# Eight subtractions given to GpSimd, and one weight rounding moved by a few products

## The chip, the core and the metric

The kernel runs on one core of one Trainium2 chip. The metric is the device time of one execution in microseconds (us). The kernel before took 1075.73 us, the median of three runs (1075.58 to 1076.07).

## What is computed

One encoder layer on 1024 tokens of width 1024, all in float32. A normed input goes through one combined projection into two kinds of attention; their outputs are normed and projected; then comes a gated feed-forward with a small convolution over the tokens, and a last norm. Cut to what matters:

```
hn = rmsnorm(h, norm_mix)
qa, ka, va, qb, kb, vb = split(hn @ w_in)
o_a = window_gqa_sink(rope(qa), rope(ka), va, sink)      # |i-j| <= 128, 8 heads
o_b = neighbourhood_attention(qb, kb, vb, rpb)           # 16 x 64 grid, 8 heads
h  = h + concat(rmsnorm(o_a, norm_a), rmsnorm(o_b, norm_b)) @ w_out
hn = rmsnorm(h, norm_ffn)
g  = conv3(hn @ w_gate) + conv_b
h  = h + (silu(g) * (hn @ w_up)) @ w_down
out = rmsnorm(h, norm_final)
```

## The kernel before

Everything lies transposed: features on the 128 partitions, tokens along a row. A tile of 128 features by 1024 tokens is worked on in two halves of 512 tokens.

**Split numbers.** Each float32 operand of a matmul is split into a high half (`whi`, `ph`, the first half of `hg`), which ScalarE rounds by a copy, and a low half (`wlo`, `pl`, the second half of `hg`), which VectorE forms as the original minus the high half. A product then takes three matmuls: high weight by high input, high weight by low input, low weight by high input (`block`, L169 to L172; `group`, L957 to L961). In the feed-forward a group of four feature tiles makes 12 matmuls. The low weight is read by the third matmul of each three (L961).

**TensorE's order is written out by hand** (`manual_schedule`, L128): its instructions run in the order of the code. On the other engines a scheduler orders the instructions when the program is built, with help from priorities and from `issue_after` (`behind`, L145). Each engine then works through its own queue strictly in order: an instruction that waits holds up all that stand behind it. SyncE's queue (SP) issues most loads.

**Attention.** Projections of the normed input, 18 tiles of 128 columns (`Project`), run as a filler between the attention steps: `rest` (L744) is a generator that yields after each `block`, and the attention loop draws on it at set rates. A tile's weights come as two raw tiles of four blocks. The first is rounded in `load` (L558), at the start of the tile before. The second is rounded in `load_rest` (L562); `rest` calls it for the next tile when the running tile has done `REST` = 11 further blocks (L757). The tiles are rounded by `halve_w` (L158): one ScalarE copy (L162) and one VectorE subtraction (L163). For the last tile, m = 17, `halve_w` gets `held`, so that both are issued behind the softmax weights' latest split (marks "high" and "rest", L417 and L418). This tile takes its eight blocks in another order (L575 to L581): for each k both token halves, so it yields 16 times and needs the second four weights from its ninth block on. After it come the eight tiles of the output projection's first part (`OutA`), which begin with rounding their own weights.

In the attention steps VectorE, ScalarE and GpSimd share the softmax: VectorE adds the bias and takes the row's minimum (L403), ScalarE takes the exponential (L407), GpSimd scales (L411), TensorE transposes (L517), ScalarE and VectorE split the result (L417, L418), and TensorE multiplies by the values (L528, L529). GpSimd also prepares the bias tiles (L481, L482).

**Feed-forward.** Gate and up projections are computed for feature tiles `f` (`Gated`, L1090) by a scheme of Strassen's kind: seven products in place of eight, on sums of the 2 x 2 blocks of weights and of the normed input. The input's blocks are (feature tiles 0 to 3 or 4 to 7) by (first or second 512 tokens); `at(k, h)` is feature tile k, half h. The products are `p1` and `p2` (plain blocks), `p5`, `p6`, `p3`, `p7` (sums "s1", "s2", "s4", "s3" of the weights) and `p4` ("22"). The input's sums are formed in place in `at(k, 0)` and `at(k, 1)` of the tiles 0 to 3:

```
B["t1"]:  sub(at(k, 1), at(k, 1), at(k, 0))       # L1181, read by p5
B["t2"]:  sub(at(k, 1), at(k + 4, 1), at(k, 1))   # L1191, read by p6
t3:       sub(at(k, 0), at(k, 1), at(k, 0))       # L1198, read by p7
t4:       sub(at(k, 1), at(k + 4, 0), at(k, 1))   # L1199, read by p4
```

Each sum is split by `operand` (L963 to L968: a ScalarE copy, L966, and a VectorE subtraction, L967). The fourth sum overwrites the second, so it has to wait until the second's operand has been formed. `sub` (L998) is a VectorE subtraction of 128 x 512 elements.

The first four units (`HEAD`, L1170 to L1220) run product by product: all p5, all p6, all p3, all p7, all p4. Their weight sums are formed in turn (`head_weights`, L1002, with `sub` too) and rounded by `split_w` (L943: ScalarE copy L948, VectorE subtraction L949). Results leave the accumulators by VectorE (L1110 for p5, L1117 for p6, L1121 for p3, L1134 for p7, L1139 for p4), and the convolution takes a ScalarE pass and two VectorE passes per unit (L1127 to L1130). Raw weights come through three buffers, rounded weights through nine (L946, L953). From the fifth unit on a loop (L1290) does the seven products of one unit after the other, with the next unit's weights prepared step by step (`Weights`, L1045).

The loop is followed by the down projection, again by seven products, and the final norm, in which GpSimd takes two of the tiles (L1384).

Of the kernel before, what the change touches and what calls it, by code (L numbers as in the profile page):

```python
# [16 lines left out]
ALU = mybir.AluOpType  # L17
# [22 lines left out]
REST = 11  # L40
# [13 lines left out]
def hybrid_layer(tc, xT, w_first, w_in, w_out, w_gate, w_up, w_down, small, sink, rpb, consts, rope, out):  # L54
    nc = tc.nc
    with ExitStack() as ctx:
# [88 lines left out]
        def behind(*names):  # L145

            stack = ExitStack()
            for n in names:
                stack.enter_context(tc.issue_after(mark[n].ins))
            return stack  # L150
# [7 lines left out]
        def halve_w(raw, held=False):  # L158

            hi, lo = (wpool.tile([128, 4, 128], F32R, name=n, tag=n) for n in ("whi", "wlo"))  # L160
            with behind(*["high", "rest"] * held):
                mark["weights"] = nc.scalar.activation(hi, raw, AF.Copy)  # L162
                mark["weights low"] = nc.vector.tensor_tensor(lo, raw, f32(hi[:, :, :]), op=ALU.subtract)  # L163
            return [(hi[:, j, :], lo[:, j, :]) for j in range(4)]
# [389 lines left out]
        class Project:  # L554
# [5 lines left out]
                self.w = halve_w(raw)  # L560

            def load_rest(self):  # L562
                self.w += halve_w(self.raw, self.m == 17)

            def run(self):
                self.t = tmp("t")
# [50 lines left out]
        xg, first = [None] * KT, [Project(m) for m in range(3)]  # L617
        third = first[2]
        jobs = [Project(m) for m in range(3, 18)] + [OutA(d) for d in range(KT)]

        def split_x(k, part=slice(0, S)):

            g, src = col(C_NMIX + k), xts[k][:, part]
            hi, lo = (t[:, part] for t in xg[k])
            pin(nc.scalar.activation(hi, src, AF.Copy, scale=g))
            pin(nc.vector.scalar_tensor_tensor(lo, src, g, f32(hi), op0=ALU.mult, op1=ALU.subtract))  # L626
# [54 lines left out]
        for part in range(3):  # L681
            for p, ps in zip(first, banks):
                w, x = p.w[0], xg[0]
# [38 lines left out]
        def make_stacks(job):  # L722
            with tc.high_priority(offset=400):
                stacks(job.m, job.t)
            done.add(job.m)

        def settle(age):

            for item in list(later):
                item[0] -= 1  # L730
                if item[0] <= 0:
                    later.remove(item)
                    item[1]()
            while waiting and (len(waiting) > 1 or age >= (LATE if waiting[0].m == 3 else SOON if waiting[0].m == 17 else LAG)):
                m = waiting[0].m
                if live["op"] + needs(m) > slots["op"]:
                    break
                live["op"] += needs(m)
                with behind(*["stack", "low"] * (m == 3)):
                    waiting.pop(0).post()  # L740
# [3 lines left out]
        def rest():  # L744
            for i, job in enumerate(jobs):
                if i + 1 < len(jobs):
                    with behind(*[["spread", "root"], ["stack"]][i] if i < 2 else []):
                        jobs[i + 1].load()
                for n, _ in enumerate(job.run()):
                    yield True  # L750
                    if i == 0:
                        if n == 8:
                            with behind("copied"):
                                for p in first[:2]:
                                    make_stacks(p)
                        continue
                    if n == REST and i + 1 < len(jobs):  # L757
                        jobs[i + 1].load_rest()
                    settle(n)
                    if (i, n) in aux:  # L760
                        aux[i, n]()
                if i == 0:
                    with behind("stack", "copied"):
                        jobs[1].load_rest()
                    with behind("weights", "weights low"):
                        make_stacks(third)
                if isinstance(job, Project):
                    waiting.append(job)
                while len(waiting) > 2:
                    settle(0)  # L770
                    if len(waiting) > 2:
                        yield False
# [29 lines left out]
        for i in range(8):  # L802
            aux[13, 1 + i + i // 2] = normed_a(*divmod(i, 2))
        filler = rest()
        live["op"] = sum(needs(m) for m in range(3))

# [115 lines left out]
        for h in range(2):  # L922
            wide = widen(vb2[h], "pt")
            for i in range(4):
                x = mix[4 + i][:, tsl(h)]
# [48 lines left out]
        at = lambda k, h: h1[k][:, tsl(h)]  # L974
# [20 lines left out]
        HEAD = 4  # L995
        FH = FT // 2
        FO = [f for k in range(FH) for f in (k, k + FH)]
        sub = lambda o, x, y: nc.vector.tensor_tensor(o, x, y, op=ALU.subtract)  # L998

        wsum = [fpool.tile([128, 4, 128], F32, name="ws", tag="tt", bufs=6) for _ in range(HEAD)]  # L1000

# [193 lines left out]
            head_weights(i, "s2")  # L1195
        B[2, 2] = [operand(at(k, 1), "op") for k in K2]
        for k in K1:
            sub(at(k, 0), at(k, 1), at(k, 0))  # L1198
            sub(at(k, 1), at(k + 4, 0), at(k, 1))  # L1199
        for i, u in enumerate(units):  # L1200
            u.p6()
            head_weights(i, "s4")
# [212 lines left out]
        for i, (p, j, c) in enumerate(order):  # L1415
# [4 lines left out]
            f, n = PARTS[c]  # L1420
# [146 lines left out]
```

## Time and profile before

| | |
|---|---|
| median of 3 runs | 1075.73 us |
| the profiled execution | 1076.77 us, of which the span of its instructions is 1075.0 us |
| busy: TensorE | 1063.8 us (99% of the span) |
| VectorE | 867.3 us (81%) |
| ScalarE | 555.7 us (52%) |
| GpSimd | 106.8 us (10%) |
| mean granted TensorE clock | 0.997 |

How the views are read. A row of the timeline has the start, the duration, the engine (PE is TensorE, PEld its weight loads, DVE is VectorE, ACT ScalarE, POOL GpSimd, SP SyncE), the line, the operation, what it writes and reads with shapes, how often it follows itself, and in brackets the engine's idle time before it and what ended it. Matmuls are pipelined: their starts tell the pace, not their durations. VectorE's instructions overlap a little as well: a subtraction of 128 x 512 lasts 0.69 us and the next one starts 0.60 us after it. A row of the waits has who waited for whom, the total in us, how often, and the longest. A row of a window has the busy time of TensorE, of its weight loads, of VectorE, ScalarE and GpSimd in that stretch, each with its number of instructions, then the granted clock, the share of time the DMA engines moved data, and GB/s. A row of the groups has how often, the busy time and the mean in ns, then the idle time before. A row of the DMA issues has how many, their size, and the median us from issue to landing.

### The profile page before, as it was taken

How to read it: one execution, taken by the hardware profiler on the slowest of the kernel's cores; microseconds unless marked ns; L12 is line 12 of the kernel's file. 1: busy time of each engine (PE TensorE's matmuls, PEld its weight loads, DVE VectorE, ACT ScalarE, POOL GpSimd, SP SyncE). 2: the span in 40 equal slices, each digit the busy share in tenths (PEclk: the TensorE clock that was granted, in tenths of full speed). 3: DMA queues.
4: the chain of work that ended last, by engine and by line, in shares of the span. 5: the costliest groups of instructions: out<-in, count | busy, mean ns of one | idle time of the engine just before them, and what ended most of it. 6: DMA issues, size and time to landing. Idle time of an engine off the chain costs nothing.

```text
span 1075.0 us, 14902 instructions
## 1 busy us (share of the span) xinstructions
PE 1063.8 (99%) x5094; PEld 889.6 (83%) x5094; DVE 867.3 (81%) x1596; ACT 555.7 (52%) x1059; POOL 106.8 (10%) x188
## 2 busy tenths in 40 slices
PE   9999999999999999999999999999999999999997
PEld 7888888888888888887788888888888888888887
DVE  7889887768878799899988877887887858897765
ACT  8457776647676554534434343432434645544451
POOL 1124333222332000000000000000000000000002
PEclk9999999999999999999999999999999999999998
DMA  7223122322234245214342232322222788867644
GB/s 278 74 74 80 40 69 60 89 69 79 78 88 148 96 156 210 78 56 162 135 157 98 106 110 81 129 106 108 98 89 101 251 288 308 270 216 241 222 139 157
DMA packets 68220, 144.94 MB, mean 135 GB/s; under 512 B 8240, under 2 KB 18736, under 8 KB 68144
## 3 DMA queue, kind: packets, MB, share of 16 engines
q1 hardware_dynamic: 57920, 118.69, 34.9%
q10 hardware_dynamic: 10224, 25.30, 6.2%
q8 instruction: 40, 0.66, 0.2%
q14 instruction: 36, 0.29, 0.1%
HBM read 103.58 MB, written 28.57 MB: 123 GB/s over the span
## 4 chain that ended last, share of the span: by engine, by line
PE 89%; DVE 7%; ACT 1%; issue 1%; DMA 1%; POOL 0%; SPq 0%; DVEq 0%; ACTq 0%
PE pj L170 8%; PE pj L172 8%; PE pj L171 8%; PE dn L959 7%; PE dn L961 7%; PE dn L960 7%; PE z L961 5%; PE z L959 5%; PE z L960 5%; PE s L381 3%; PE x L959 3%; PE x L961 3%; PE x L960 3%; PE y L961 3%; PE y L959 3%; PE y L960 3%
## 5 line engine op out<-in xcount | busy, mean ns | idle before, releaser
L948 ACT ACTIVATE whi<-ws 128x512 fp32r<-128x512 f32 (+1 forms) x100 | 60.3, 623 | 126.8 <-DVE ws L1066 82.5
L959 PE MATMUL dn<-xd,whi 128*128 128x512 f32 (+1 forms) x330 | 124.0, 376 | 0.0
L961 PE MATMUL dn<-xd,wlo 128*128 128x512 f32 (+1 forms) x330 | 123.7, 375 | 0.0
L960 PE MATMUL dn<-xd,whi 128*128 128x512 f32 (+1 forms) x330 | 123.7, 375 | 0.0
L961 PE MATMUL z<-hg,wlo 128*128 128x512 f32 x264 | 103.1, 390 | 0.9 <-DVE wlo L949 0.7
L170 PE MATMUL pj<-xgh,whi 128*128 128x512 f32 x245 | 103.3, 422 | 0.0
L959 PE MATMUL z<-hg,whi 128*128 128x512 f32 x264 | 103.0, 390 | 0.0
L960 PE MATMUL z<-hg,whi 128*128 128x512 f32 x264 | 102.8, 389 | 0.0
L407 ACT ACTIVATE p<-p,nm 128x385 f32<-128x385 f32 (+3 forms) x128 | 75.2, 587 | 50.8 <-DVE nm L403 49.7
L411 POOL TENSOR_SCALAR p<-p,sm 128x384 f32<-128x384 f32 (+1 forms) x128 | 78.1, 622 | 207.2 <-DVE sm L409 171.7
L171 PE MATMUL pj<-xgl,whi 128*128 128x512 f32 x245 | 96.2, 393 | 0.3 <-DVE xgl L626 0.3
L172 PE MATMUL pj<-xgh,wlo 128*128 128x512 f32 x245 | 96.4, 393 | 0.0
L949 DVE TENSOR_TENSOR wlo<-raw,whi 128x512 fp32r<-128x512 f32 (+1 forms) x102 | 66.4, 671 | 26.6 <-ACT whi L948 25.6
L418 DVE TENSOR_TENSOR pl<-pt,ph 128x384 fp32r<-128x384 f32 (+2 forms) x108 | 63.5, 589 | 24.9 <-ACT ph L417 23.5
L948 ACT ACTIVATE whi<-raw 128x512 fp32r<-128x512 f32 (+1 forms) x102 | 60.5, 612 | 44.6 <-DMA raw<-in_w_down_dram 19.8
L949 DVE TENSOR_TENSOR wlo<-ws,whi 128x512 fp32r<-128x512 f32 (+1 forms) x100 | 67.0, 683 | 19.1 <-ACT whi L948 17.9
L1384 POOL TENSOR_TENSOR h<-h,wide 128x256 f32<-128x256 f32 (+1 forms) x6 | 5.4, 918 | 707.4 <-ACT wide L1380 707.4
L417 ACT ACTIVATE ph<-pt 128x384 fp32r<-128x384 f32 (+2 forms) x108 | 55.2, 512 | 32.4 <-PE pt L517 24.7
L961 PEld LDWEIGHTS dn<-xd,wlo 128*128 128x128 f32 x330 | 62.1, 188 | 11.2
L960 PEld LDWEIGHTS dn<-xd,whi 128*128 128x128 f32 x330 | 62.1, 188 | 11.2
L959 PEld LDWEIGHTS dn<-xd,whi 128*128 128x128 f32 x330 | 62.1, 188 | 10.9
L1274 ACT ACTIVATE xd<-xd 128x512 fp32r<-128x512 f32 x77 | 47.6, 626 | 43.8 <-DMA xd<-x 42.1
(270 smaller groups left out, 2678.0 us busy)
## 6 DMA issues: line engine op xcount, KB each, us to landing
xd<-x SPq DMA_DIRECT2D x77, 256.0 KB, 4.8
raw<-in_w_down_dram SPq DMA_DIRECT2D x72, 256.0 KB, 3.8
raw<-in_w_gate_dram SPq DMA_DIRECT2D x22, 512.0 KB, 3.5
raw<-in_w_up_dram SPq DMA_DIRECT2D x22, 512.0 KB, 3.9
x<-c ACTq DMA_DIRECT2D x22, 512.0 KB, 3.3
raw<-in_w_in_dram SPq DMA_DIRECT2D x30, 256.0 KB, 2.8
raw<-in_w_down_dram SPq DMA_DIRECT2D x36, 192.0 KB, 4.2
x<-t ACTq DMA_DIRECT2D x11, 512.0 KB, 2.7
```

Source lines behind the costliest of these rows:

```text
L170: nc.tensor.matmul(ps, w[0], x[0][:, tsl(h)], start=first, stop=False)
L171: nc.tensor.matmul(ps, w[0], x[1][:, tsl(h)], start=False, stop=False)
L172: nc.tensor.matmul(ps, w[1], x[0][:, tsl(h)], start=False, stop=last)
L407: nc.scalar.activation(p[:, j, 0:e], p[:, j, 0:e], AF.Exp, bias=nm, scale=-1.0, accum_out=sm[:, j:j + 1])
L411: nc.gpsimd.tensor_scalar(p[:, i, 0:m], p[:, i, 0:m], sm[:, i:i + 1], 1.0, op0=ALU.mult, op1=ALU.mult)
L417: mark["high"] = nc.scalar.activation(ph[:, 0:n], ps[:, 0:n], AF.Copy)
L418: mark["rest"] = nc.vector.tensor_tensor(pl[:, 0:n], ps[:, 0:n], f32(ph[:, 0:n]), op=ALU.subtract)
L948: nc.scalar.activation(hi, src, AF.Copy)
L949: nc.vector.tensor_tensor(lo, src, f32(hi[:, :, :]), op=ALU.subtract)
L959: nc.tensor.matmul(ps, w[0], x[0], start=first and i == 0, stop=False, skip_group_check=True)
L960: nc.tensor.matmul(ps, w[0], x[1], start=False, stop=False, skip_group_check=True)
L961: nc.tensor.matmul(ps, w[1], x[0], start=False, stop=last and i == len(ws) - 1, skip_group_check=True)
```

## The change

Two edits that have nothing to do with each other. The third and fourth sums of the normed input, eight subtractions, are issued on GpSimd instead of VectorE. And the second weights of the last projected tile (m = 17, `jobs[14]`) are rounded when that tile has done three of its own blocks (n = 2), no longer at the twelfth block of the tile before it, and without the `held` order.

```
             def load_rest(self):
-                self.w += halve_w(self.raw, self.m == 17)
+                self.w += halve_w(self.raw)
...
         jobs = [Project(m) for m in range(3, 18)] + [OutA(d) for d in range(KT)]
+        last_in = jobs[14]
...
-                    if n == REST and i + 1 < len(jobs):
+                    if n == REST and i + 1 < len(jobs) and jobs[i + 1] is not last_in:
                         jobs[i + 1].load_rest()
+                    if n == 2 and job is last_in:
+                        job.load_rest()
                     settle(n)
...
-        sub = lambda o, x, y: nc.vector.tensor_tensor(o, x, y, op=ALU.subtract)
+        sub = lambda o, x, y, engine=nc.vector: engine.tensor_tensor(o, x, y, op=ALU.subtract)
...
         for k in K1:
-            sub(at(k, 0), at(k, 1), at(k, 0))
-            sub(at(k, 1), at(k + 4, 0), at(k, 1))
+            sub(at(k, 0), at(k, 1), at(k, 0), nc.gpsimd)
+            sub(at(k, 1), at(k + 4, 0), at(k, 1), nc.gpsimd)
```

Besides, the scheduler places the instructions around both edits anew: VectorE's, ScalarE's and SyncE's queues differ from the kernel before near them, and in the feed-forward up to the seventh unit or so. TensorE's order is the same.

## The prediction

> Line numbers are those of the kernel before; times are us from the start of the profiled span.
>
> **What bounds the kernel now.** I read the page's first part, then TensorE's waits in the two stretches that the diff touches.
>
> ```profile
> PE 1063.8 (99%) x5094; PEld 889.6 (83%) x5094; DVE 867.3 (81%) x1596; ACT 555.7 (52%) x1059; POOL 106.8 (10%) x188
> ```
>
> ```profile
> PE o L529 <- DVE pl L418: 0.9, 1, 0.9
> ```
>
> ```profile
> PE z L961 <- DVE wlo L949: 0.7, 2, 0.4
> PE y L961 <- DVE wlo L949: 0.5, 2, 0.3
> ```
>
> The first wait row is 250 to 320 (attention), the others are 440 to 540 (the head of the feed-forward). TensorE is busy 99% of the span, so only its pauses can be won. What the pauses cost is read from TensorE's starts (timeline):
>
> ```profile
> 453.40 0.39 PE L959 MATMUL y<-hg,whi 128*128 128x512 f32 x1
> ...
> 464.28 0.39 PE L959 MATMUL z<-hg,whi 128*128 128x512 f32 x1
> ...
> 486.04 0.39 PE L959 MATMUL z<-hg,whi 128*128 128x512 f32 x1
> ...
> 494.40 0.39 PE L961 MATMUL z<-hg,wlo 128*128 128x512 f32 x1
> 494.71 0.50 PE L959 MATMUL z<-hg,whi 128*128 128x512 f32 x1
> 495.05 0.40 PE L960 MATMUL z<-hg,whi 128*128 128x512 f32 x1
> 495.78 0.50 PE L961 MATMUL z<-hg,wlo 128*128 128x512 f32 x1 [0.34 <-DVE wlo L949]
> 496.12 0.39 PE L959 MATMUL z<-hg,whi 128*128 128x512 f32 x1
> ...
> 532.73 0.39 PE L959 MATMUL z<-hg,whi 128*128 128x512 f32 x1
> ```
>
> From 453.40 to 464.28 are four products of 12 matmuls: 10.88, so 2.72 a product and 0.227 a matmul. From 486.04 to 532.73 are 16 products, 43.53 at that pace; they took 46.69. So this stage loses 3.16, in five pauses like that at 495: the wait, and about 0.2 besides, since the steps around it are 0.31 and 0.34 instead of 0.227. Each pause waits for a low half of a weight from VectorE. VectorE has no idle time in front of them, where the sums stand, and little between them:
>
> ```profile
> 465.00:470.00 5.00, 5.00 (x24) 4.14 (x23) 5.00 (x9) 3.07 (x5) 0.00 (x0) 1.00 0.00 0
> 495.00:500.00 5.00, 4.66 (x21) 3.49 (x20) 4.13 (x8) 2.07 (x4) 0.00 (x0) 1.00 0.62 192
> ```
>
> (After the colon and the sum: TensorE, weight loads, VectorE 5.00 of 5.00, ScalarE, GpSimd idle, clock 1.00.)
>
> **The sums: what goes.**
>
> ```profile
> 453.90 1.89 DVE L998 TENSOR_TENSOR h<-h,h 128x512 f32<-128x512 f32 x3
> 455.70 1.89 DVE L967 TENSOR_TENSOR hg<-h,hg 128x512 fp32r<-128x512 f32 x3
> 457.51 0.69 DVE L998 TENSOR_TENSOR h<-h,h 128x512 f32<-128x512 f32 x1
> ...
> 464.71 0.70 DVE L1110 TENSOR_TENSOR c<-y,c 128x512 f32<-128x512 f32 x1
> 465.31 1.30 DVE L998 TENSOR_TENSOR h<-h 128x512 f32<-128x512 f32 x2
> ...
> 470.13 0.70 DVE L1117 TENSOR_TENSOR gs<-z,c 128x512 f32<-128x512 f32 x1
> ```
>
> The eight sums (L1198, L1199) stand from 465.31 to 470.13: 4.82, or 0.60 each. VectorE would gain 4.8 if nothing else changed, more than any single pause.
>
> **What comes.** Eight instructions on GpSimd, of a kind that the trace shows at this size:
>
> ```profile
> L1384 POOL TENSOR_TENSOR h<-h,wide 128x512 f32<-128x512 f32 x2 | 2.6, 1296 | 691.9 <-ACT wide L1380 691.9
> ```
>
> They take 1.30 each, 10.4 in all. GpSimd is empty until that row, so nothing queues behind them there. In the changed program's order the first three need only the second sums (453.90 on), so GpSimd starts near 455, not at 465: beside VectorE's work, not after it. What that does is shown where GpSimd's L481 and L482 met VectorE in attention:
>
> ```profile
> 248.17 0.99 POOL L481 TENSOR_TENSOR xb<-cst,rr 128x384 f32<-128x384 f32 x1 [1.18 <-DVE nm L403]
> 249.12 1.17 POOL L482 TENSOR_TENSOR xb<-cst,rr 128x256 f32<-128x256 f32 x1
> ```
>
> ```profile
> 248.22 1.50 DVE L163 TENSOR_TENSOR wlo<-raw,whi 128x512 fp32r<-128x512 f32 x1
> 249.63 1.21 DVE L299 SCALAR_TENSOR_TENSOR kb<-t,cst,ka 128x512 fp32r<-128x512 f32 x1
> ```
>
> And the same forms where they did not meet (the last row is for the rounding, below):
>
> ```profile
> 294.55 0.99 POOL L481 TENSOR_TENSOR xb<-cst,rr 128x384 f32<-128x384 f32 x1 [0.37 <-DVE nm L403]
> 295.50 0.72 POOL L482 TENSOR_TENSOR xb<-cst,rr 128x256 f32<-128x256 f32 x1
> ```
>
> ```profile
> 295.57 0.54 DVE L418 TENSOR_TENSOR pl<-pt,ph 128x384 fp32r<-128x384 f32 x1
> ...
> 301.51 0.69 DVE L163 TENSOR_TENSOR wlo<-raw,whi 128x512 fp32r<-128x512 f32 x1
> ...
> 306.29 0.42 DVE L418 TENSOR_TENSOR pl<-pt,ph 128x256 fp32r<-128x256 f32 x1 [0.83 <-ACT ph L417]
> ```
>
> L163 took 1.50 instead of 0.69 and ended 0.56 after L481's end; L482 then took 1.17 instead of 0.72 and ended 0.57 after L163; L299 ended 0.55 after L482. They went strictly in turn. An instruction on GpSimd holds VectorE up for its own time less 0.15 (0.72 against 0.57). L418, which reads PSUM, ran at 0.54 beside L482: it wasn't held.
>
> So a sum on GpSimd costs a VectorE instruction with both inputs in SBUF 1.30 - 0.15 = 1.15. That is dearer than the 0.60 which it removes. From 455.10 VectorE has 17 instructions up to 465.31, all but four (L1110, which read PSUM) with two inputs in SBUF. Taken in turn: GpSimd 455.05 to 456.20, VectorE to 456.75, and so on, eight rounds of 1.15 + 0.55, with two of L1110 beside GpSimd. VectorE comes to the place of 465.31 at 465.31 + 8 x 1.15 - 2 x 0.60 - 8 x 0.05 (0.55 against 0.60) = 472.9, say 473.0, against 470.13 now: **2.9 late instead of 4.8 early**. Bounds: 465.3 if no instruction is held, 474.5 if L1110 is held too.
>
> The Trainium skill, page "SBUF — State Buffer", section "Who interferes with whom", states that VectorE and GpSimd share a port pair as an exclusive lock, taken by a VectorE instruction with two SBUF inputs against a GpSimd instruction that reads SBUF, and that the later one blocks fully. The trace agrees on the turns (0.56, 0.57 and 0.55 behind each other) and differs on the length: by the page's wording the whole 1.30 would be held, 1.2 more over eight sums, and the time would be 1079.9; by the rows it is 1.15.
>
> **What is late then.** I walk the changed program's order with 0.60 for an instruction, 1.20 for each conv pass (L1128, L1129) and 0.76 from a VectorE start to the matmul that reads it:
>
> ```profile
> 495.05 0.68 DVE L949 TENSOR_TENSOR wlo<-ws,whi 128x512 fp32r<-128x512 f32 x1
> ```
>
> (its matmul: 495.78 above). Weights come back by
>
> ```profile
> raw<-in_w_gate_dram SPq DMA_DIRECT2D x22, 512.0 KB, 3.5
> ...
> raw<-in_w_up_dram SPq DMA_DIRECT2D x8, 256.0 KB, 3.1
> ```
>
> 1. The second sums' last low half (L1192, k = 3) stands behind seven of the holds: it ends at 466.95 and is readable at 467.05; its matmul is due at 464.28 + 10 x 0.227 = 466.55: 0.5 lost. On ScalarE's queue the same operand's high half stands behind three copies that now wait for GpSimd (third sums 0 and 1, fourth sum 0, the last done at 461.3); its own input comes at 463.6, so that new wait hides.
> 2. Fifteen instructions from 473.0 bring VectorE to the first s3 weight sum (L1015) at 482.0. The low halves of the third sums stand among them and find GpSimd done (468.2): no wait. From there to the third unit's s3 low half stand twelve instructions of 0.60 and four conv passes of 1.20, and two waits: 0.9 until the second unit's raw weights are there (buffer free at 482.7, 3.1 to load), 0.3 for ScalarE. 482.0 + 7.2 + 4.8 + 1.2 = 495.2, readable at 495.95. TensorE's s3 products (L1133) start at 486.04 + 0.5 = 486.6; the third unit's needs it at 486.6 + 2 x 2.72 + 0.45 = 492.5: 3.45 lost. The fourth unit's is due at 498.7 and comes at 498.95: 0.25.
> 3. The next unit's gate weights start to load when the buffer of a "22" weight is free, at 501.7, and land at 505.2; VectorE stands behind them for 1.9. The walk brings it to the low half of the second loop unit's s1 at 532.65, readable at 533.4, due at 531.55: 1.85.
>
> Lost: 0.5 + 3.45 + 0.25 + 1.85 = 6.05, and 0.2 for each of four pauses, 6.85. Now 3.16 is lost. The sums cost **+3.7**. After that unit the walk finds every low half ready, as the trace of before does up to the kernel's end part. If VectorE were only 1 late at 473, item 2 would shrink by 1.9.
>
> **The rounding.** It moves one ScalarE copy and one VectorE subtraction (L162, L163), no DMA. In the changed order they follow the first output weights' rounding, near 307 and 308.3. Now the copy stands at 300.85 and the subtraction at 301.51 (above):
>
> ```profile
> 300.85 0.62 ACT L162 ACTIVATE whi<-raw 128x512 fp32r<-128x512 f32 x1
> ...
> 304.05 0.96 ACT L417 ACTIVATE ph<-pt 128x384 fp32r<-128x384 f32 x2
> ```
>
> ```profile
> 304.14 0.38 PE L517 MATMUL pt<-cst,p 128*128 128x128 f32 x2
> 304.59 0.44 PE L528 MATMUL o<-ph,v 128*128 128x384 f32 x1
> 305.18 0.44 PE L529 MATMUL o<-pl,v 128*128 128x384 f32 x1
> 305.46 0.38 PE L517 MATMUL pt<-cst,p 128*128 128x128 f32 x2
> ```
>
> From 304.14 to 305.46 is 1.32; two transposes of 0.11 and two of 0.18 are 0.58. So 0.74 goes, because ph (304.05) leaves before the second exponential instead of behind it. In the new place VectorE's 0.83 of idle time at 306.29 covers the subtraction, and the weights are needed only eight blocks of three matmuls into that tile, 5.4 after its start. On SP one output-weight load moves behind a q copy; it belongs to the second output tile, a whole tile later. If that cover failed, up to 0.7 would come back. The 0.9 pause at 286 is another instruction's and stays.
>
> Sum: 1076.77 (span 1075.0 and 1.77 around it) + 3.7 - 0.7 = 1079.8; against the median 1075.73: **1078.7**.
>
> **Rivals.** *No collision* (faster): the sums run beside VectorE at no price. Then it is 4.8 early from 465 on, the 3.16 go, and 1075.73 - 3.16 - 0.74 = 1071.8; half of it, 1073.5. It decides if a hold costs under 0.60; for it speaks only a meeting like 295.57, where VectorE read PSUM. Chance 0.15. *Collision absorbed*: VectorE loses 1 to 3, but the new order brings critical halves earlier, and the pauses stay near 3 to 4: 1075 to 1076.5. For it: VectorE idles 0.87 in 495 to 500. Chance 0.2. *Deeper delay*: L1110 is held too (474.5), and each later load starts later; 1.5 more at three places, 1082 to 1083. Chance 0.1. That the rounding isn't moved far enough to matter leaves 1079.4, inside the forecast's own range.
>
> **How the numbers follow.** Forecast 1078.7, chance 0.55, with its own range 1077 to 1080.5. A measurement tells 0.2%, 2.15, from no change: 1073.6 to 1077.9. Faster: 0.14 of the first rival and 0.02: 0.16. Same: 0.10 of the forecast, 0.15 of the absorbed case, 0.01: 0.26. Slower: 0.58. The range 1073.5 to 1081.5 leaves out most of the first rival's best half and the deepest delay, under 0.2.
>
> **What would show it.** The eight sums on GpSimd between 455 and 469 at 1.3 to 1.9 each; VectorE instructions of 0.69 drawn out to about 1.8 beside them, L1110 not; the gs of 470.13 near 473; a pause of 3 to 4 near 493 under L961, waiting for wlo; a smaller one near 531; no pause at 304. VectorE at 0.69 throughout would make it wrong, and so would a pause under 1 near 493.

## The result and the profile after

| | before | after |
|---|---|---|
| median of 6 runs each | 1076.03 us (1075.58 to 1076.82) | 1082.05 us (1081.51 to 1083.67) |
| ratio | 1 | 1.0059 (95%: 1.0048 to 1.0069) |
| span of the profiled execution | 1075.0 us | 1080.4 us |

The change makes the kernel 6.0 us slower. The forecast was 3.0 slower (1078.7) with a range up to 1081.5: the side is right, the size is half, and the time lies above the range.

In the lines of the kernel after, everything from the diff's second place on stands three lines lower (L949 is L952, L961 is L964, L967 is L970, L998 is L1001, L1110 is L1113, L1117 is L1120). The page's first part:

```profile
PE 1063.3 (98%) x5094; PEld 889.5 (82%) x5094; DVE 866.4 (80%) x1588; ACT 555.3 (51%) x1059; POOL 122.6 (11%) x196
```

VectorE has eight instructions less and is busy for only 0.9 less: what the eight sums gave back went into other instructions, drawn out. TensorE runs the same 5094 matmuls in the same order in both kernels, so the start of a matmul after, minus the start of the same matmul before, tells where time is lost:

```
matmul                  before    after    difference
ss, end of the start      32.06    31.13    -0.93
ahead of the rounding    300                -0.82
behind the rounding      310                -1.52
s, a new wait            316.61   316.05    -0.56
behind that wait         320                -0.45
y, first p3              475.61   476.20    +0.59
z, third unit's p7       491.90   494.81    +2.90
z, the same unit later   495.78   500.19    +4.41
y, first unit of loop    521.30   527.15    +5.86
one of the last         1068.68  1074.19    +5.51
```

The first 0.9 is from the kernel's start, which no edit touches; the runs below show it between -0.2 and -1.0. The rounding gains 0.70 at 304 and gives 1.07 back at 316. From there to 527 the feed-forward loses the rest, 6.3, of which the next 10 us give 0.3 back. TensorE's waits from 440 to 560, after (total, how often, longest):

```profile
PE y L962 <- DVE c L1113: 2.8, 1, 2.8
PE z L962 <- ACT whi L951: 2.4, 1, 2.4
PE y L964 <- DVE wlo L952: 0.6, 1, 0.6
PE z L964 <- DVE wlo L952: 0.5, 1, 0.5
```

Before, all waits here were for low halves from VectorE. Now the two long ones are for a high half from ScalarE and for an accumulator that VectorE has not read yet. And from 250 to 320, after, beside the wait of 0.9 at 286 that stays:

```profile
PE s L381 <- DMA kb<-ka: 0.8, 1, 0.8
```

No such wait is there before. Now what the sums did. GpSimd's timeline after (start, duration):

```profile
454.28 4.61 POOL L1001 TENSOR_TENSOR h<-h 128x512 f32<-128x512 f32 x1 [96.56 <-DVE h L1001]
...
460.55 1.30 POOL L1001 TENSOR_TENSOR h<-h 128x512 f32<-128x512 f32 x1
```

ScalarE's timeline after:

```profile
458.93 0.63 ACT L969 ACTIVATE hg<-h 128x512 fp32r<-128x512 f32 x1 [2.82 <-POOL h L1001]
460.63 0.63 ACT L969 ACTIVATE hg<-h 128x512 fp32r<-128x512 f32 x1 [1.07 <-POOL h L1001]
463.13 1.15 ACT L969 ACTIVATE hg<-h 128x512 fp32r<-128x512 f32 x2 [1.87 <-POOL h L1001]
...
491.88 1.28 ACT L1133 ACT_TABLE_LOAD   x1
493.18 1.06 ACT L1133 ACTIVATE cv<-cv 128x1024 f32<-128x1024 f32 x1
494.14 0.61 ACT L951 ACTIVATE whi<-ws 128x512 fp32r<-128x512 f32 x1
```

And VectorE's timeline after:

```profile
457.66 0.68 DVE L1113 TENSOR_TENSOR c<-y,c 128x512 f32<-128x512 f32 x1
...
464.31 1.82 DVE L970 TENSOR_TENSOR hg<-h,hg 128x512 fp32r<-128x512 f32 x1 [4.87 <-ACT hg L969]
...
473.07 1.88 DVE L1001 TENSOR_TENSOR ws<-raw,ws 128x512 f32<-128x512 f32 x3
474.88 0.68 DVE L1120 TENSOR_TENSOR gs<-z,c 128x512 f32<-128x512 f32 x1
```

Read the three engines together. GpSimd's first sum starts at 454.28 and stands until 458.89, 1.23 after VectorE's start on L1113, the first instruction in its run that reads PSUM. Three of ScalarE's copies wait for GpSimd in turn. Behind the third of them (463.13, the first half of the x2 row) stands the high half of the last second sum, so VectorE, whose next instruction is that operand's low half, idles for 4.87 (464.31). While VectorE idles, GpSimd's sums take 1.30; when it is back, its instructions take 1.82. The ws subtractions at 473.07 follow on the same instruction on which the sums at 465.31 followed before, and the first p6 result (gs), at 470.13 before, is read at 474.88, since three of these subtractions now stand ahead of it.

What TensorE makes of it, after, is in its starts:

```profile
491.98 0.39 PE L964 MATMUL z<-hg,wlo 128*128 128x512 f32 x1
494.81 0.50 PE L962 MATMUL z<-hg,whi 128*128 128x512 f32 x1 [2.44 <-ACT whi L951]
...
496.02 0.79 PE L964 MATMUL z<-hg,wlo 128*128 128x512 f32 x1 [0.48 <-DVE wlo L952]
496.61 0.63 PE L962 MATMUL z<-hg,whi 128*128 128x512 f32 x1
...
523.99 0.39 PE L964 MATMUL x<-hg,wlo 128*128 128x512 f32 x1
527.15 0.50 PE L962 MATMUL y<-hg,whi 128*128 128x512 f32 x1 [2.77 <-DVE c L1113]
```

and in the windows (TensorE's busy time, weight loads, VectorE, ScalarE, GpSimd, then the granted clock):

```profile
492.00:494.00 2.00, 0.37 (x2) 0.00 (x0) 2.00 (x3) 1.99 (x2) 0.00 (x0) 1.00 0.21 53
494.00:496.00 2.00, 0.73 (x2) 0.30 (x2) 2.00 (x4) 1.30 (x3) 0.00 (x0) 0.86 0.55 209
496.00:498.00 2.00, 1.98 (x5) 1.60 (x6) 2.00 (x4) 1.26 (x3) 0.00 (x0) 0.50 0.00 0
498.00:500.00 2.00, 2.00 (x9) 1.59 (x8) 2.00 (x4) 0.41 (x1) 0.00 (x0) 0.78 0.75 254
...
526.00:528.00 2.00, 0.85 (x4) 0.72 (x5) 2.00 (x4) 0.60 (x1) 0.00 (x0) 1.00 0.73 285
```

The pause at 492 costs more than its length. Behind it the clock is granted at 0.50, and matmuls start every 0.427 instead of 0.227 until 499.04. From 491.98 to 499.04 are ten steps, 2.27 at full pace; they took 7.06, so 4.79 is lost, of which 1.43 behind 496.02 is the clock's. The pause at 524 is longer, and the clock stays at 1.00 behind it.

### The profile page after: what moved, and what is told of

It reads as the page before. It is cut to its first block, busy times and chain, and to the rows that moved or that the text cites. A ratio compares the mean times of both kernels' runs of the same rounds, so it can differ in the third digit from the quotient of the medians.

```text
span 1080.4 us, 14917 instructions
## 1 busy us (share of the span) xinstructions
PE 1063.3 (98%) x5094; PEld 889.5 (82%) x5094; DVE 866.4 (80%) x1588; ACT 555.3 (51%) x1059; POOL 122.6 (11%) x196
## 4 chain that ended last, share of the span: by engine, by line
PE 87%; DVE 7%; DMA 3%; ACT 2%; issue 1%; POOL 0%; SPq 0%; DVEq 0%; ACTq 0%
PE pj L170 7%; PE pj L172 7%; PE pj L171 7%; PE dn L962 6%; PE dn L964 6%; PE dn L963 6%; PE z L962 4%; PE z L963 4%; PE z L964 4%; PE x L963 3%; PE x L964 3%; PE x L962 3%; PE s L381 3%; PE y L962 3%; PE y L963 3%; PE y L964 3%
## 5 line engine op out<-in xcount | busy, mean ns | idle before, releaser
L964 PE MATMUL dn<-xd,wlo 128*128 128x512 f32 (+1 forms) x330 | 123.7, 375 | 0.0
L964 PE MATMUL z<-hg,wlo 128*128 128x512 f32 x264 | 103.4, 392 | 0.5 <-DVE wlo L952 0.5
L952 DVE TENSOR_TENSOR wlo<-raw,whi 128x512 fp32r<-128x512 f32 (+1 forms) x102 | 66.5, 671 | 30.7 <-ACT whi L951 29.8
L952 DVE TENSOR_TENSOR wlo<-ws,whi 128x512 fp32r<-128x512 f32 (+1 forms) x100 | 69.0, 701 | 19.2 <-ACT whi L951 17.9
L964 PEld LDWEIGHTS dn<-xd,wlo 128*128 128x128 f32 x330 | 62.1, 188 | 11.3
L962 PE MATMUL y<-hg,whi 128*128 128x512 f32 x176 | 68.6, 390 | 2.8 <-DVE c L1113 2.8
L963 PEld LDWEIGHTS dn<-xd,whi 128*128 128x128 f32 x330 | 62.1, 188 | 11.1
```

What stands on the lines that cost most here:

```text
L952: nc.vector.tensor_tensor(lo, src, f32(hi[:, :, :]), op=ALU.subtract)
L962: nc.tensor.matmul(ps, w[0], x[0], start=first and i == 0, stop=False, skip_group_check=True)
L963: nc.tensor.matmul(ps, w[0], x[1], start=False, stop=False, skip_group_check=True)
L964: nc.tensor.matmul(ps, w[1], x[0], start=False, stop=last and i == len(ws) - 1, skip_group_check=True)
```

## The experiments

In the diffs and rows of this section the line numbers are those of the kernel before. Two theories were at stake for the feed-forward. **A, the queue**: the overshoot comes from ScalarE's order, which leaves VectorE idle for 4.87. **B, the port**: GpSimd's sums hold VectorE for as long in any order, and the idle time only stands where holds would stand. Each expectation is quoted as it was written before the run.

**1. The sums alone.** The diff's `sub` and L1198, L1199, without the rounding.

> Only the first edit: the eight sums on GpSimd, the rounding where it was. If the two edits add up, the time is that of the changed kernel's feed-forward stage alone: TensorE's starts there fall back from 0.56 ahead of the kernel before to 5.54 behind it, 6.1 us, so 1082.1. Rival: the moved rounding costs a part of the 6.0 (a wait of 0.8 for a DMA at 315 is new in the changed kernel), then this run stays at 1081 or below.

Measured: 1084.14 (1082.61 to 1085.75), before 1076.56; ratio 1.007 (1.0056 to 1.0084), +7.6. So the sums cost all of the loss; the moved rounding takes nothing from it that can be told (the interval overlaps that of both edits together). In this execution the second pause, too, has slow steps behind it:

```profile
524.34 0.39 PE L961 MATMUL x<-hg,wlo 128*128 128x512 f32 x1
527.17 0.80 PE L959 MATMUL y<-hg,whi 128*128 128x512 f32 x1 [2.45 <-DVE c L1110]
527.76 0.63 PE L960 MATMUL y<-hg,whi 128*128 128x512 f32 x1
```

These slow steps cost 1.7 in this execution, which is most of what the run lies above the kernel after.

**2. The rounding alone.** L563, L619, L757 of the diff only.

> Only the second edit: the rounding moved, the sums on VectorE. TensorE's starts in the changed kernel gain 0.6 at 304 and give 0.9 back at 315, where the first half of a stacked key tile comes late by DMA. If that wait belongs to the edit, the time is 1076.0 + 0.3 = 1076.3, no difference that can be told. Rival: the wait at 315 is chance of that one execution, then 1075.3.

Measured: 1076.98 (1076.26 to 1078.04), before 1076.56; ratio 1.0004 (0.9995 to 1.0013). The wait is there again, from 250 to 320 in this run:

```profile
PE s L381 <- DMA kb<-ka: 0.7, 1, 0.7
```

TensorE gains 0.68 at 304 (its start minus that before goes from -0.53 to -1.21) and gives 0.98 back at 316 (to -0.23). So the wait belongs to the edit, and the edit is worth nothing that can be told.

**3. One copy earlier on ScalarE**, in the run with the sums alone:

```
     operand:  nc.scalar.activation(...)   ->   mark["copy"] = nc.scalar.activation(...)
...
             B["t2"].append(operand(at(k, 1), "xg")); mark["second"] = mark["copy"]
...
         with behind("second"): B["t3"] = [operand(at(k, 0), "op") for k in K1]
...
             with behind("second"): B["t4"].append(...)
```

> As the run with the first edit alone, but ScalarE's copy of the last second sum (the fourth of t2) stands ahead of the copies that wait for GpSimd, not behind three of them; no other instruction of any engine changes its place. Theory A (the queue): VectorE's idle 4.9 us at 459 to 464 comes from that copy and goes; VectorE reaches the first p6 result at 472 to 473 instead of 474.9, and the time is 2 to 2.5 below the run with the first edit alone, 1079.5 to 1080. Theory B (the port): without the idle time GpSimd's sums hold VectorE just as long, one after the other, and the time is within 0.5 of the run with the first edit alone.

Measured: 1081.4 (1080.95 to 1082.4); ratio 1.0045 (1.0032 to 1.0057), 2.7 below run 1. The drop is near A's 2 to 2.5, though the time is above A's 1079.5 to 1080, since run 1 itself came out 2 above its expectation; VectorE's place is nearer to B's. VectorE's timeline in this run:

```profile
453.56 0.68 DVE L998 TENSOR_TENSOR h<-h,h 128x512 f32<-128x512 f32 x1
...
459.49 1.78 DVE L967 TENSOR_TENSOR hg<-h,hg 128x512 fp32r<-128x512 f32 x1
461.18 0.68 DVE L1110 TENSOR_TENSOR c<-y,c 128x512 f32<-128x512 f32 x1
461.78 1.18 DVE L949 TENSOR_TENSOR wlo<-ws,whi 128x512 fp32r<-128x512 f32 x1
...
473.79 0.68 DVE L1117 TENSOR_TENSOR gs<-z,c 128x512 f32<-128x512 f32 x1
```

From the first second sum to the first p6 result VectorE takes 20.23; in run 1 it takes 21.45, by these two rows:

```profile
453.01 0.68 DVE L998 TENSOR_TENSOR h<-h,h 128x512 f32<-128x512 f32 x1
...
474.46 0.68 DVE L1117 TENSOR_TENSOR gs<-z,c 128x512 f32<-128x512 f32 x1
```

The 4.87 of idle time goes, and 3.7 of it comes back as holds: every instruction with two inputs in SBUF now takes 1.78 (or 1.18, where L1110 stood beside the first part of the sum), L1110 stays at 0.68. So B holds for three quarters of VectorE's delay. What the 1.2 that is left was worth, TensorE's starts in the two traces show place by place: 1.2 at 466 and 475, where run 3 has no pause any more; and 2.4 at 524, where the pause is 1.98 instead of 2.83 and no slow steps follow. At 491 run 3 loses 1.0 more than run 1, as the slow steps there last twice as long. So the 2.7 is VectorE's 1.2 and, for the rest, where the clock happened to fall in these executions.

**4. Only the fourth sums on GpSimd** (L1198 back on VectorE).

> As the first edit, but only the four fourth sums on GpSimd; the third sums stay on VectorE. The fourth can start only when the third have been formed, near 466, when the second sums' operands are done, so no urgent copy stands behind them on ScalarE, and VectorE has less two-input work beside them. Theory A: VectorE saves 2.4, is held for up to four times 1.15, and is 0 to 2 late behind it: 1076 to 1078. Theory B: half of the sums costs half of the loss, 1079.

Measured: 1078.71 (1077.63 to 1079.68), before 1076.56; ratio 1.0018 (1.0009 to 1.0027), +2.2: between the two numbers. Half of the sums cost less than a third of run 1's 7.6. The first sum again stands until VectorE reads PSUM. GpSimd in this run, and VectorE:

```profile
465.61 2.82 POOL L998 TENSOR_TENSOR h<-h,h 128x512 f32<-128x512 f32 x1 [107.97 <-DVE h L998]
```

```profile
467.19 0.68 DVE L1117 TENSOR_TENSOR gs<-z,c 128x512 f32<-128x512 f32 x1
467.79 4.61 DVE L998 TENSOR_TENSOR ws<-raw,ws 128x512 f32<-128x512 f32 x3
```

465.61 + 2.82 = 468.43 is 1.24 after 467.19, as 458.89 was 1.23 after 457.66. The three ws subtractions, 1.88 in a row in the kernel after (473.07), take 4.61.

**5. The rounding two blocks later**, sums on VectorE (n counts from 0):

```
-                    if n == 2 and job is last_in:
+                    if n == 4 and job is last_in:
```

> Only the second edit, but the rounding two blocks later (when the last projected tile has done five blocks, not three). VectorE then works both halves of the key's low part (L299) ahead of the rounding's subtraction, and on SyncE an output-weight load stands behind the four stacked-tile copies. Theory: the wait at 315 for the copy of a key half came from that second half of L299, 1.5 us behind the first; it goes here, the gain of 0.6 to 0.7 at 304 stays, TensorE's starts stay 0.6 ahead from 304 on, and the time is 1075.9. Rival: the copy is bound by the transfers themselves (3 us for two in a row); then the wait at 315 stays whole, as TensorE still comes there 0.6 earlier.

Measured: 1075.86 (1074.79 to 1077.38), before 1076.3; ratio 0.9997 (0.9988 to 1.0005). The time can't tell 0.4 from nothing, the trace can: TensorE gains 0.68 at 304 (its starts go from -0.11 at 300 to -0.79 at 310), holds it until 488 (-0.82) and is at -0.61 at the last, and the wait for the stacked tile is gone. What was in its way, in run 2 (VectorE):

```profile
307.69 0.74 DVE L299 SCALAR_TENSOR_TENSOR kb<-t,cst,ka 128x512 fp32r<-128x512 f32 x1
...
309.52 0.73 DVE L299 SCALAR_TENSOR_TENSOR kb<-t,cst,ka 128x512 fp32r<-128x512 f32 x1
```

Before, the second L299 starts 0.66 behind the first, here 1.83: the rounding's L163 and two others are ahead of it. Run 5 moves back both that half and, on SyncE, an output-weight load (L155) that stood between the stacked-tile copies. SyncE's timeline in run 2 tells the two apart:

```profile
308.06 0.53 SPq L155 DMA_DIRECT2D raw<-in_w_out_dram  x1
310.29 0.47 SPq L302 DMA_DIRECT2D q<-kb  x1
...
313.30 0.46 SPq L303 DMA_DIRECT2D kb<-ka  x1
```

The load is issued by 308.6, but the copy q<-kb only at 310.29, 0.03 after the second L299 ends, and kb<-ka, for which TensorE waits, is issued when q<-kb has landed, 3.0 later. So it was the key half. With the load out of the way, in run 5, those two copies are 3.3 apart (308.94 and 312.24), not closer.

**6. The fourth sums issued later, on VectorE**, with run 5's rounding:

```
         for k in K1:
             sub(at(k, 0), at(k, 1), at(k, 0))
-            sub(at(k, 1), at(k + 4, 0), at(k, 1))
...
         for k in K1:
+            sub(at(k, 1), at(k + 4, 0), at(k, 1))
             B["t4"].append(operand(at(k, 1), "mix" if k else "rstd"))
```

> As the run before this one, and the fourth sums stay on VectorE but are issued where the third products are done, not behind the third sums: VectorE's queue loses 2.4 us of work ahead of the s4 and s3 weights and has it later. Theory: what the head of the feed-forward loses (3.16 us in five pauses) is VectorE's order there, so two or three of the pauses go, 1 to 2 us, and the time is 1074 to 1075, below both kernels. Rival: the second operand chain and the raw weights' transfers (a load that lands at 493) bound the same stage, the pauses stay near 3, and the time is 1076.

Measured: 1074.53 (1074.11 to 1076.11), before 1076.3; ratio 0.9985 (0.9977 to 0.9994), 1.8 below the kernel before. Of the five pauses the two at 489 and 495 are gone, and the next one, near 511, has grown (its longest step from 0.57 to 1.04); TensorE's waits from 440 to 560 in this run:

```profile
PE y L961 <- DVE wlo L949: 0.9, 2, 0.7
PE z L961 <- DVE wlo L949: 0.4, 1, 0.4
```

**7. Filler in the pause.** The kernel after, and ahead of the third unit's p7 twelve matmuls with a weight of zeros:

```
+    [nc.tensor.matmul(self.z, zero, B["t3"][j % 4][0], start=False, stop=False, ...)
+     for j in range(12 * (self.f == FO[2]))]
     group(self.z, W[self.f, "s3"], B["t3"], False, True)
```

> The changed kernel, and ahead of the third unit's p7 product twelve more matmuls with a weight of zeros (they add nothing): 2.7 us of work for TensorE that waits for nothing, in the pause of 2.8 at 492. Theory: the seven slow steps behind that pause (0.427 instead of 0.227) are the granted clock, which fell because TensorE idled; with the filler the clock stays at 1.00, the steps are 0.227, and the kernel gains 1.2 to 1.4. Rival: the steps are slow for another reason (weights late, loads on the same memory); then they stay, and the time does not move.

Measured: 1084.8 (1083.2 to 1088.1), before 1076.3; ratio 1.0081 (1.0069 to 1.0094), 8.5 above before, where the changed kernel is 6.0 above it. The windows of this run:

```profile
492.00:494.00 2.00, 2.00 (x10) 1.65 (x10) 2.00 (x3) 1.97 (x3) 0.00 (x0) 1.00 0.00 0
...
496.00:498.00 2.00, 1.52 (x7) 1.12 (x7) 2.00 (x5) 1.15 (x2) 0.00 (x0) 1.00 0.01 3
498.00:500.00 2.00, 2.00 (x9) 1.35 (x8) 2.00 (x4) 1.07 (x2) 0.00 (x0) 1.00 0.49 168
...
530.00:532.00 2.00, 2.00 (x6) 1.52 (x6) 1.97 (x4) 0.00 (x0) 0.00 (x0) 0.50 0.10 39
```

The mechanism holds: with the filler the clock stays at 1.00, and from the product's first matmul (495.46, after 494.81) to 499 TensorE gains 1.3 on the kernel after, within the expected 1.2 to 1.4. The time does not follow. The extra matmuls made the scheduler place VectorE's and ScalarE's work anew from 502 on: a step of 1.71 at 521 is new and costs 1.5, and the pause at 525, as long as that at 524 in the kernel after (3.18 and 3.16), now has slow steps behind it, which cost 1.6. As a test of the clock it is good, as a test of the time it isn't clean.

**8 and 9. Is it the port?** The kernel before, with 26 GpSimd instructions beside the same stretch that nobody waits for: subtractions of a constant's slices, or fills with zeros.

```
+    junk[:, 0:8] = at(0, 1)[:, 0:8] - at(0, 1)[:, 8:16]            # starts them at 454, in both
+    26 x  nc.gpsimd.tensor_tensor(junk, cst[:, 0:128], cst[:, 128:256], op=ALU.subtract)
or
+    26 x  nc.gpsimd.memset(junk, 0.0)
```

> The kernel before, all sums on VectorE, and 26 extra GpSimd subtractions of two 128x128 slices of a constant into a scratch tile that nobody reads, from the first second sum on (about 454). No instruction waits for them, and the order of VectorE and ScalarE is that of before. Theory (the port): VectorE's instructions with two inputs in SBUF are drawn out beside them, each by about one GpSimd instruction less 0.15, those that read PSUM are not, and GpSimd's first one stands until VectorE reaches an instruction that reads PSUM. Rival: what drew VectorE out in the changed kernel was waiting for data; then every VectorE instruction stays at 0.69.

> As the run with the 26 subtractions, but GpSimd fills the scratch tile with zeros 26 times: it writes SBUF and reads nothing. If reading is what takes turns with VectorE, VectorE's instructions stay at 0.69 and the time is that of before; if any GpSimd access to SBUF does, they are drawn out as in the run before this one.

Measured in one run each: 1082.59 with the readers and 1075.78 with the writers, before 1077.32 beside them. Readers, GpSimd and VectorE:

```profile
454.94 3.59 POOL L1189 TENSOR_TENSOR junk<-h 128x8 f32<-128x8 f32 x1 [97.17 <-DVE h L998]
```

```profile
458.38 0.69 DVE L1110 TENSOR_TENSOR c<-y,c 128x512 f32<-128x512 f32 x1
...
461.60 0.95 DVE L949 TENSOR_TENSOR wlo<-ws,whi 128x512 fp32r<-128x512 f32 x1
462.47 0.94 DVE L967 TENSOR_TENSOR hg<-h,hg 128x512 fp32r<-128x512 f32 x1
```

Writers, VectorE, at the same place:

```profile
462.10 1.29 DVE L967 TENSOR_TENSOR hg<-h,hg 128x512 fp32r<-128x512 f32 x2
```

The order of VectorE's and ScalarE's instructions in this stretch is that of the kernel before in both runs. Reading GpSimd instructions alone, with no queue behind them and (but for the eight elements of the first) no data in common, draw VectorE out (0.95 for 0.69) and cost 5.3; writing ones draw nothing out (1.29 for two in a row is 0.69 and a start 0.60 later). So the collision is over reading SBUF. The first instruction has 8 elements a partition and still stands for 3.59, until L1110.

**10. The deferred fourth sums on GpSimd** (run 6 with `nc.gpsimd` in the new line).

> As the run with the deferred fourth sums, but these four are issued on GpSimd in that later place. Theory: wherever VectorE works mostly on two inputs in SBUF, a sum on GpSimd holds it for about 1.15 and spares it 0.60, so the stage gets four times 0.5 dearer at VectorE, pauses of 1 to 2 come back, and the time is 1075.5 to 1077. Rival: late sums are off every critical path (read only by the fourth products), so that GpSimd costs nothing here; then the time is that of the deferred sums on VectorE, 1074.5.

Measured: 1077.84 (1077.4 to 1078.52), before 1076.33; ratio 1.001 (1.0002 to 1.0019), 3.3 above run 6 and over the top of the expectation. The rival falls, and the theory was put wrongly: the sums did not run late. GpSimd in this run:

```profile
465.01 2.81 POOL L998 TENSOR_TENSOR h<-h,h 128x512 f32<-128x512 f32 x1 [107.99 <-DVE h L998]
```

Its queue is empty, so it starts as soon as the data are there, at 465 as in run 4. On an idle engine the place in the code delays nothing.

**11. Deferred sums without the rounding.**

> Only the deferred fourth sums on VectorE, the rounding as in the kernel before. The trace of the run with both gave 1.3 in the feed-forward and 0.6 in attention; if these add, this one gives 1075.0. Rival: the gain in the feed-forward hangs on TensorE's coming there 0.6 earlier; then less than half of it stays, 1075.8.

Measured: 1075.46 (1074.88 to 1076.97), before 1076.33; ratio 0.9995 (0.9986 to 1.0004), between the two numbers, and by the time alone not told from the kernel before. In the trace TensorE gains 0.8 between 488 and 532 (from -0.55 to -1.33), and in run 6 it gains 0.8 there as well (from -0.95 to -1.72), less than the 1.3 of the expectation. That speaks against the rival, and the two gains add within what can be told (run 6 is 1.8 below before, runs 5 and 11 are 0.4 and 0.9 below).

## Why the prediction was right in its side and wrong in its size

Three steps of the prediction failed: that ScalarE's new wait behind GpSimd hides; that what is late then is only the weights it walked to, at the price of the wait and 0.2 each; and that the moved rounding is covered. Lost against TensorE's pace, place by place (after: steps between starts, less 0.227 each; the prediction's pauses with their restarts):

```
place                 predicted            after
466, second sums        0.7                 0.2
475, first s4 weight    0                   0.9
493, third unit's s3    4.1 (3.45+0.25+0.4) 4.8
524 / 531, the loop     2.05                3.0
sum                     6.85                8.9   (before 3.16)
the rounding           -0.74               +0.37  (-0.70 at 304, +1.07 at 316)
```

- **What bounds the kernel** held: every difference is a pause of TensorE.
- **The price of a sum**: 1.15 a hold, in turn, with instructions that read PSUM free, is what run 3 shows (1.78 is 0.60 and 1.18). VectorE was to come to the place of 465.31 at 473.0; it came at 473.07, or at 473.5 by the prediction's clock, since the whole stretch began 0.45 earlier (the first second sum at 453.45, not 453.90). But it got there by another way, fewer holds and 4.87 of idle time, so that the two came out nearly alike is luck. The sign "gs near 473" failed (474.88) for a smaller reason: three subtractions stand ahead of it in the changed order. **"That new wait hides" is a step that failed**: the copies were to be free at 461.3, the last one waited until 463.1, because the first sum stood for 4.61 and not 1.15. By run 3 this wait is worth 1.2 at VectorE, and 2.7 in time as the clock fell there.
- **"Strictly in turn" failed for the first sum**: an unbroken run of VectorE does not let GpSimd in.
- **What is late then** failed in its size. The walk from 473.0 to the third unit's s3 low half is right in its steps: the first s3 weight sum came at 482.09 (482.0 predicted), with 0.92 of waiting for raw weights behind it (0.9), the low half at 495.28 (495.2), and its matmul starts at 496.02 (readable at 495.95). Three things were left out: the high half of the same weight, which stood on ScalarE behind the table load and a silu and came at 494.81 (it cost nothing more, since the low half came later); the clock (1.43 behind this pause, where 0.2 a restart was taken, though the prediction let TensorE stand for 3.45 there); and the first s4 weight, which the walk passed without asking when it was due (0.9). The pause at 531 came at 524 as another wait: not a weight but an accumulator that VectorE had not read, 3.0 instead of 2.05.
- **The rounding**: the pause at 304 went as said, 0.70 instead of 0.74. **"Covered" failed**: VectorE's gap covered the subtraction, but the rounding stood in front of a key half and its stacked copies, 1.07 at 316 that the prediction's bound (up to 0.7) did not see, since it asked only when the rounded weights are due and not who is queued behind them.

The mis-sized terms add up to the miss. In the sums they are 0.9 at 475, 0.7 at 493 and 1.0 at 524, less 0.5 at 466, together 2.1; in the rounding 1.1. That is 3.2, and the miss is 3.0 by the differences to the kernel before (6.0 against 3.0) and 3.4 by the times (1082.05 against 1078.7). The rival that came nearest is *deeper delay* (1082 to 1083, chance 0.1), with a wrong mechanism: L1110 was not held. Asking of every pause over 2 what the clock does behind it would have given that price more chance. Three small slips in the prediction's working change nothing: from VectorE's start to the matmul its own rows give 0.73, not 0.76; half of the first rival's gain is 1073.8, not 1073.5; and with L1110 held its sum gives 474.1, not 474.5.

## What to carry to other kernels

Before moving work to an idle engine, ask whether the two engines will have to take turns at reading memory: here a GpSimd subtraction that spared VectorE 0.60 held it for about 1.15, while GpSimd instructions that only write held nothing. Walk the queue of every engine that waits for the moved work, ask who stands behind it, and remember that an engine with an empty queue starts early wherever the line stands. The same four sums, left on VectorE and only issued when their readers are near, gained 0.8 in two traces, where moving them to GpSimd lost 2.2 in time (run 4).

## What the runs showed of the hardware

**A run of VectorE keeps GpSimd out.** In the six runs with sums on GpSimd (after, 1, 3, 4, 7 and 10) the first sum ended 1.23 to 1.24 after the start of VectorE's first instruction that reads PSUM, whether it had stood for 3.4 or 1.6 before that; in runs 8 and 9 the first instruction, of 8 elements a partition, stood for 3.59 and ended 0.15 after the start of that VectorE instruction. Once GpSimd is in, the two alternate (run 3). The Trainium skill, page "SBUF — State Buffer", section "Who interferes with whom", has it that the one that starts first gets the pair for the whole instruction and that GpSimd's writes alone do not contend. The second agrees with runs 8 and 9; to the first these runs add that VectorE's instructions, back to back, pass the pair on to each other.

**A pause slows the clock behind it, by how much of it falls into one window.** By TensorE's starts, steps of 2.83 (after), 3.25 and 2.83 (run 1), 3.36 (run 3) and 3.18 (run 7) were followed by 3 to 6.6 us of steps of 0.427, some of them after a second pause of 0.9 right behind the first (after, and the first of run 1); so was one of 1.95 with another of 0.90 right behind it (run 8). One of 3.16 (after, at 524) and those of 1.98 (run 3) and 1.71 (run 7) were not. The Trainium skill, page "TensorE: Matmul & The Clock Gate", section "What's actually happening", has a monitor with a window of 3.4 us that runs freely; that the same length of pause falls out both ways fits it, and pauses well under a window were enough here.

The traces' record of the granted clock shows the windows themselves. From its first rise on, every stretch of it up to the kernel's end part is a whole multiple of 3.413 us (run 1: 491.52 at full clock, 3.41 at half, 27.31 at full, 3.41 at half). In the 3.41 us ahead of each of the six drops TensorE was idle for 2.05 (run 8) to 2.79 (run 7); in no other window of that grid, from 20 to 1060 in all the thirteen traces, was it idle for more than 1.79. The pause of 2.83 at 492 lies in one window, which has 2.44 of idle time; the longer one of 3.16 at 524 is cut by the edge at 526.18 into 1.79 and 0.98. So what counted in these runs is the idle time within one window: by these traces, a pause of 2 to 3 us slows the clock or not by where the windows' edges fall.
